# Two-layer decoder trunk, first pass: order of the loads, place of the casts, place of the bias rows

## The chip, the cores and the metric

The kernel runs on one core of one Trainium2 chip. The metric is the device time of one launch in microseconds (us), the median of several runs. The engines of the core are TensorE (PE; its weight loads are PEld), VectorE (DVE), ScalarE (ACT), GpSimd (POOL) and SyncE (SP). SP issues most DMA transfers, GpSimd the others; both kinds run on the core's 16 DMA engines (queue q1 holds SP's, q0 GpSimd's).

## The reference

Two layers, each with a token mixer and a gated convolutional FFN, each sub-layer normed and modulated by vectors that come from a conditioning vector c. The part that matters here is the beginning of layer 0:

```python
mod = jax.nn.silu(c) @ w_ada[0] + b_ada[0]
sh1, sc1, g1, sh2, sc2, g2 = [m[:, None, :] for m in jnp.split(mod, 6, axis=-1)]
h = rmsnorm(x, norm_mix[0]) * (1.0 + sc1) + sh1
qkv = (h @ w_in).reshape(B, S, A_GROUPS, 3, A_HEADS, A_HEAD_DIM)   # 1024 -> 9216
# per group and head: dilated causal attention with a bias that a table
# rel_bias gives by distance; then the mixture of the groups, the output
# projection, the FFN, and layer 1 with gated linear attention
```

There are 256 tokens of width 1024. All is float32.

## The kernel before

Products are made of float32 numbers in three: each operand is split into a high part (a cast to the type that TensorE multiplies fast, on ScalarE) and a low part (the rest, a subtraction on VectorE), and high x high, low x high and high x low are added up in PSUM. A weight chunk is therefore loaded (tile raw), cast (whi), subtracted (wlo), and then multiplied.

The model's width is cut into eight tiles of 128 (kt = 0 to 7). The **first pass** (lines 391 to 478, and the products at 679 to 709) goes over these eight tiles once. For a tile it
- loads the tile's ada chunk (1 MB, two pieces up to kt = 3, else one; L415) and its chunk of w0, the input weights of the first two pairs of heads (0.98 MB, also in two pieces up to kt = 3: 768 and 1152 columns; L418). Chunks of odd tiles go to one fixed room (early_x), all other loads share a ring of four buffers (wraw), so that a load waits on SP until the buffer's last reader is done;
- makes two dot products of the ada chunk with silu(c) on VectorE (L161). On ScalarE the first becomes the scale m1 (L170), the second the shift m0 (L172);
- scales x by m1 and the norm's factor on VectorE (xr, L432), adds m0 on ScalarE, which gives the high part hhi (L436), and takes the low part hlo on VectorE (L440);
- casts w0's two column pieces on ScalarE (L448, the first between m1 and m0, the second behind the high part) and subtracts their low parts on VectorE (L453);
- multiplies on TensorE, 36 products of 256 columns and 6 of 384 (L690, L686), in a written order: high x high first, which needs both casts; the pieces with wlo last.

The order on ScalarE and on VectorE is written out: each step stands behind the one before it (`behind`, with the lists on_act and on_dve; it orders instructions of one engine and adds no wait on another). A tile's steps on VectorE are dot, dot, scale, first low part, hlo, second low part. Where no order is written, a planner sets it before the launch; so it is for SP's queue. What SP and GpSimd issue goes in the order of their queues: an issue that waits for a buffer holds all behind it.

Behind the pass ScalarE and VectorE empty the banks (L597 and L598 the first pair, whose bank TensorE writes next). TensorE goes on with a chunk of query and key weights (wqk, whole products by parts, L654; its casts at L191), then scores, and a chunk of value weights (wv). 

GpSimd builds the table rows of biases (L370); at the end of the pass SP stores it to DRAM (rows_d, L479) and loads the rest of small (L480). From there GpSimd loads each pair of heads' bias, eight copies of 64.5 and 32 KB in turn (L384, L385, in short runs of up to 1 KB); the first two pairs have buffers at once. In its queue behind these stand two room loads (L495) of 1 MB ada chunks for later, to the rooms early_x and x_all, which are free when tile 7's dots and scaling are done. At most eight of GpSimd's transfers are in flight in this stretch.

Of the kernel before, what the change touches and what calls it, by code (L numbers as in the profile page):

```python
# [57 lines left out]
def trunk(ctx: ExitStack, tc: tile.TileContext, I, out):  # L58
    nc = tc.nc
# [12 lines left out]
    def bank(name="ps", tag=None):  # L72
        tag = tag or next(cycle)
        return psum.tile([P, 512], F32, tag=tag, name=name, bufs={"p": 2, "s": 4, "t": 2}[tag])
# [44 lines left out]
    @contextmanager  # L119
    def behind(*those):  # L120

        with ExitStack() as st:
            for i in those:
                st.enter_context(tc.issue_after(i.ins))
            yield
# [29 lines left out]
    def modulation(raw, l, n, order=(0, 1), between=None):  # L155
        first = ()
        for s in order:
            piece, kt = ADA_ORDER[2 * n + s]
            dot = tmp.tile([P, 1], F32, tag="dot", name="dot", bufs=4)
            w = raw[:, D * s : D * s + D]  # L160
            last_dot[0] = nc.vector.tensor_tensor_reduce(  # L161
                w, w, c_bc, op0=ALU.mult, op1=ALU.add, scale=1.0, scalar=0.0, accum_out=dot,
            )
            m = state.tile([P, 1], F32, tag=f"mod{l}{piece}{kt}", name="mod")
            b = col(C_BADA + 48 * l + 8 * piece + kt)
            with behind(*first):
                if piece in (1, 4):
                    g = col((C_NMIX if piece == 1 else C_NFFN) + 8 * l + kt)
                    b1 = (16 if piece == 4 else 0) + 8 * l + kt
                    last = nc.scalar.activation(m, dot, AF.Identity, scale=g, bias=one_b[:, b1 : b1 + 1])  # L170
                else:
                    last = nc.scalar.activation(m, dot, AF.Identity, bias=b)  # L172
            mod[l, piece, kt] = m
            if between and s == order[0]:
                first = between(last)
        return last


    last_load, copied, last_lo = [None], [None], [None]

    def split(src, n, dmas=1, after=((), ()), late=(), low=()):
        raw = wraw.tile([P, 2048], F32, tag="raw", name="raw")
        for i in range(dmas):
            c = slice(n * i // dmas, n * (i + 1) // dmas)
            last_load[0] = nc.sync.dma_start(raw[:, c], src[:, c])
        hi = wspl.tile([P, 2048], F32R, tag="whi", name="whi")
        lo = wspl.tile([P, 2048], F32R, tag="wlo", name="wlo")
        for i in range(0, n, n // 2):
            c = slice(i, i + n // 2)
            with behind(*after[i > 0]):  # L190
                copied[0] = nc.scalar.copy(hi[:, c], raw[:, c])  # L191
        for i in range(0, n, n // 2):
            c = slice(i, i + n // 2)
            with behind(*(late if i else low)):
                last_lo[0] = nc.vector.tensor_tensor(lo[:, c], raw[:, c], hi[:, c].bitcast(F32), op=ALU.subtract)  # L195
        return hi, lo
# [16 lines left out]
    def mm3(ps, a, b, start, stop):  # L213


        mm(ps, a[0], b[0], start=start, stop=False)  # L216
        mm(ps, a[0], b[1], start=False, stop=False)  # L217
        return mm(ps, a[1], b[0], start=False, stop=stop)  # L218
# [137 lines left out]
    def parts(w, at, n=P):  # L356
        return w[0][:, at : at + n], w[1][:, at : at + n]
# [3 lines left out]
    rows_d = dram.tile([16, NROW], F32, name="rows_d")  # L361
# [3 lines left out]
    rows = att.tile([16, NROW], F32, tag="pt", name="rows")  # L365
# [40 lines left out]
    w0, h, xr, raw0 = [], [], [None] * KT, []  # L406
    pieces = (slice(0, 6 * P), slice(6 * P, 15 * P))
    on_act = [norm_ops[1]]

    rooms = [z.rearrange("p k t -> p (k t)")[:, 0:2048] for z in (early_all, x_all)]  # L410

    def load(kt):
        chunk = rooms[0] if kt % 2 else wraw.tile([P, 2048], F32, tag="raw", name="ada_raw")
        for c in (slice(D, 2 * D), slice(0, D)) if kt < 4 else (slice(0, 2 * D),):
            nc.sync.dma_start(chunk[:, c], I["w_ada"][0, kt][:, c])  # L415
        raw = wraw.tile([P, 2048], F32, tag="raw", name="raw")
        for c in pieces if kt < 4 else (slice(0, 15 * P),):
            last_load[0] = nc.sync.dma_start(raw[:, c], I["w0"][kt][:, c])  # L418
        raw0.append(raw)
        w0.append([wspl.tile([P, 2048], F32R, tag=f"w{part}", name=f"w{part}") for part in ("hi", "lo")])  # L420
        return chunk

    def dots(kt, between=None):
        chunk = load(kt)
        with behind(on_dve[0], on_act[0]):
            on_act[0] = modulation(chunk, 0, kt, (1, 0), between)
        on_dve[0] = last_dot[0]

    def scaled(kt):
        xr[kt] = tmp.tile([P, T], F32, tag="xr", name="xr")  # L430
        with behind(on_dve[0]):
            on_dve[0] = nc.vector.scalar_tensor_tensor(xr[kt], x[kt], mod[0, 1, kt][:, 0:1], r, op0=ALU.mult, op1=ALU.mult)  # L432

    def shifted(kt):
        with behind(on_act[0]):
            on_act[0] = nc.scalar.activation(h_hi[kt][:, :], xr[kt], AF.Identity, bias=mod[0, 0, kt][:, 0:1])  # L436
# [8 lines left out]
    def cast(kt, half):  # L445
        c = pieces[half]
        with behind(on_act[0]):
            on_act[0] = nc.scalar.copy(w0[kt][0][:, c], raw0[kt][:, c])  # L448
# [4 lines left out]
            on_dve[0] = nc.vector.tensor_tensor(w0[kt][1][:, c], raw0[kt][:, c], w0[kt][0][:, c].bitcast(F32), op=ALU.subtract)  # L453

    def tile_of(kt):
        def first_cast(last):
            on_act[0] = last
            cast(kt, 0)
            return on_act[:1]

        dots(kt, first_cast)
        scaled(kt)
        shifted(kt)
        cast(kt, 1)

    for kt in range(KT):
        tile_of(kt)
# [8 lines left out]
            low(kt, 1)  # L476
    scale_terms(1)
    with tc.issue_after(last_load[0].ins):
        nc.sync.dma_start(rows_d, rows)  # L479
        nc.sync.dma_start(small[:, C_CW:], I["small"][:, C_CW:])  # L480

    o_hi, o_lo = [], []
# [155 lines left out]
    def queries(u, g, *qk):  # L638
        pq, pk, middle, end = raw_queries(u, g, after=pt_copy[:1] if (u, g) == (3, 0) else ())
        kept[:] = evacuate(*qk, g, pq, pk)  # L640
        with behind(kept[1]):
            room_ada()
        return middle, end

    def raw_queries(u, g, tag="p", low=(), by_parts=False, after=()):
        w = split(I["wqk"][u - 2, g], 2048, low=low, late=low, after=(after, after))
        pqk = bank("pqk", tag)
        pq, pk = pqk[:, :T], pqk[:, T:]
        if by_parts:
            for part in range(3):  # L650
                for kt in range(KT):
                    for i, ps in enumerate((pq, pk)):
                        at = 2 * P * kt + P * i
                        end = mm(ps, w[part == 2][:, at : at + P], h[kt][part == 1], start=(part == kt == i == 0),  # L654
                                 stop=(part == 2 and kt == KT - 1 and i == 1))
            return pq, pk, None, end
        for kt in range(KT):
            s, e = kt == 0, kt == KT - 1
            mm3(pq, parts(w, 2 * P * kt), h[kt], s, False)
            end = mm3(pk, parts(w, 2 * P * kt + P), h[kt], False, e)  # L660
            if kt == 3:
                middle = end
        return pq, pk, middle, end
# [13 lines left out]
    last = [warm]  # L677
# [24 lines left out]
    for kt in range(1, KT):  # L702
# [4 lines left out]
        for part in (1, 2):  # L707
# [3 lines left out]
    qk0, qk1 = new_qk(), new_qk()  # L711
    left = [evacuate(*qk, g, pqk[2 * g], pqk[2 * g + 1])
            for qk, pqk, g in ((qk0, pqk0, 1), (qk0, pqk0, 2), (qk0, pqk0, 0), (qk1, pqk1, 0), (qk1, pqk1, 1), (qk1, pqk1, 2))]
    pq, pk, middle, end = raw_queries(2, 0, tag="t", low=left[2][1:], by_parts=True)
    with behind(left[-1][0], left[-3][0]):
        v0 = by_groups(pv)
    bias = load_bias(0)
# [3 lines left out]
    with behind(end):  # L721
        s, last = scores(*qk0)
# [6 lines left out]
    end = values(1, 1, pv, after=left[-1][:1], low=evacuated[1:])  # L729
# [5 lines left out]
    with behind(end):  # L735
        s, last = scores(*qk1)
    raised = maxima(s, bias1)

    for u in range(2, NPAIR):
# [3 lines left out]
        with behind(last):  # L743
            if u > 2:
                queries(u, 0, *qk)
            middle, end = queries(u, 1, *qk)
# [9 lines left out]
        middle, end = queries(u, 2, *qk)  # L756
# [5 lines left out]
        end = values(u, 0, pv, after=first)  # L762
# [3 lines left out]
        if u < NPAIR - 1:  # L766
            end = values(u, 1, pv)
        with behind(end, turned):
            s, last = scores(*qk)
        with behind(last):  # L770
            last = outputs(u - 1, v, before[1])
# [264 lines left out]
    for n in range(4):  # L1036
# [7 lines left out]
        for i in range(2):  # L1044
            kt = 2 * n + i
            for t in range(2):
                ht = [y[:, P * t : P * t + P] for y in h[kt]]
                for s in range(2):
                    with behind(*last_gate if kt == 5 else ()):
                        last = mm3(pv[t][s], ht, parts(w, D * i + 512 * s, 512), kt == 0, kt == KT - 1)  # L1050
# [18 lines left out]
    def in_turn(products):  # L1069
        with behind(*(run if run[0] else ())):  # L1070
            run[0] = products()
# [288 lines left out]
    with behind(last_pd[0]):  # L1360
        last = mean_square([0])
    with behind(last):
        last = turned(range(2))
    with behind(last):
        last = mean_square([1])
# [7 lines left out]
    for half in range(2):  # L1373
        for t, own in enumerate(halves):
            c = slice(512 * half, 512 * half + 512)
# [118 lines left out]
```

## Time and profile before

| | us |
|---|---|
| median of 3 runs (754.93 to 756.13) | 755.52 |
| the profiled execution | 754.74 |
| its span | 753.0 |
| TensorE busy (share of the span) | 745.0 (99%) |
| weight loads busy | 723.7 (96%) |
| VectorE busy | 630.5 (84%) |
| ScalarE busy | 491.5 (65%) |
| mean DMA rate | 248 GB/s |

The chain that ended last lies 88% on TensorE. The granted clock of TensorE is full throughout (2.4 GHz). A busy TensorE is not a full one: products are pipelined, and a product that waits inside still counts. So the first pass has to be read from the starts of its tiles and from the waits of the weight loads. In the first 50 us the DMA engines are full.

### The profile page before, as it was taken

The page shows a single profiled execution, that of the slowest core. Times are in us where ns is not written, and L with a number is a line of the kernel's source. Part 1 is how long each engine was busy: PE and PEld are TensorE (multiplying, and loading weights), DVE is VectorE, ACT ScalarE, POOL GpSimd, SP SyncE. Part 2 cuts the span into 40 slices and gives each one's busy share as a digit, 9 for nine tenths or more (in the row PEclk, how much of TensorE's full clock was granted, in tenths as well). Part 3 has the DMA queues.
Part 4 walks back from the last instruction along what each step waited for, and adds up shares of the span by engine and source line. Part 5 has one row for each costly group of instructions (what it writes and reads, how often), then busy time and mean ns, then how long its engine had stood idle before and what let it go on. Part 6 is the DMA issues. An engine that isn't in the chain of part 4 may idle for free.

```text
span 753.0 us, 16106 instructions
## 1 busy us (share of the span) xinstructions
PE 745.0 (99%) x6474; PEld 723.7 (96%) x6474; DVE 630.5 (84%) x1124; ACT 491.5 (65%) x954; POOL 78.2 (10%) x148
## 2 busy tenths in 40 slices
PE   9999999999999999999999999999999999999997
PEld 7999999999999999999999998899999999999996
DVE  7988977887978688999988778987897989898672
ACT  6467676576666588676766547845878766666552
POOL 6243320320200010000000002000010000000100
PEclk9999999999999999999999999999999999999999
DMA  8999788888886666866646985873475755556741
GB/s 340 417 353 369 246 297 308 292 280 280 288 282 227 235 224 220 285 225 229 241 147 229 329 315 180 340 277 130 155 279 172 277 188 204 198 181 216 266 149 56
DMA packets 31997, 186.83 MB, mean 248 GB/s; under 512 B 4386, under 2 KB 4770, under 8 KB 16051
## 3 DMA queue, kind: packets, MB, share of 16 engines
q1 hardware_dynamic: 26816, 162.38, 60.0%
q0 software_dynamic: 4784, 23.09, 9.4%
q8 instruction: 50, 0.82, 0.4%
q10 hardware_dynamic: 322, 0.35, 0.1%
q14 instruction: 25, 0.20, 0.1%
HBM read 184.70 MB, written 1.10 MB: 247 GB/s over the span
## 4 chain that ended last, share of the span: by engine, by line
PE 88%; DVE 5%; DMA 3%; ACT 2%; issue 1%; SPq 0%; ACTq 0%; DVEq 0%
PE pab L216 10%; PE pab L217 10%; PE pab L218 10%; PE pd L216 5%; PE pd L217 5%; PE pd L218 5%; PE pqk L216 5%; PE pqk L217 4%; PE pqk L218 4%; PE pv L217 3%; PE pv L218 3%; PE pv L216 3%; DMA early_x<-in_w_ada 2%; PE py L217 2%; PE py L218 2%; PE py L216 2%
## 5 line engine op out<-in xcount | busy, mean ns | idle before, releaser
L195 DVE TENSOR_TENSOR wlo<-raw,whi 128x1024 fp32r<-128x1024 f32 (+3 forms) x254 | 272.4, 1105 | 54.7 <-ACT whi L191 53.6
L191 ACT CAST whi<-raw 128x1024 fp32r<-128x1024 f32 (+3 forms) x254 | 228.6, 949 | 107.4 <-PE pab L217 40.8
L218 PE MATMUL pab<-hhi,wlo 128*128 128x256 f32 x672 | 184.9, 276 | 0.0
L217 PE MATMUL pab<-hlo,whi 128*128 128x256 f32 x672 | 184.8, 277 | 0.0
L216 PE MATMUL pab<-hhi,whi 128*128 128x256 f32 x672 | 183.4, 277 | 0.0
L218 PEld LDWEIGHTS pab<-hhi,wlo 128*128 128x128 f32 x672 | 126.2, 188 | 0.0
L217 PEld LDWEIGHTS pab<-hlo,whi 128*128 128x128 f32 x672 | 126.0, 188 | 0.2
L216 PEld LDWEIGHTS pab<-hhi,whi 128*128 128x128 f32 x672 | 125.2, 188 | 0.1
L217 PE MATMUL pd<-glo,whi 128*128 128x256 f32 x352 | 97.1, 276 | 0.0
L218 PE MATMUL pd<-ghi,wlo 128*128 128x256 f32 x352 | 97.1, 276 | 0.0
L216 PE MATMUL pd<-ghi,whi 128*128 128x256 f32 x352 | 96.8, 276 | 0.0
L216 PE MATMUL pqk<-hhi,whi 128*128 128x256 f32 x314 | 88.2, 281 | 0.0
L217 PE MATMUL pqk<-hlo,whi 128*128 128x256 f32 x314 | 87.0, 277 | 0.0
L218 PE MATMUL pqk<-hhi,wlo 128*128 128x256 f32 x314 | 87.0, 277 | 0.0
L161 DVE CUSTOM_DVE_ANT_0 ada_raw<-ada_raw,c_bc 128x1024 f32<-128x1024 f32 x52 | 61.4, 1222 | 8.2 <-DMA ada_raw<-in_w_ada 8.2
L217 PEld LDWEIGHTS pd<-glo,whi 128*128 128x128 f32 x352 | 66.1, 188 | 0.0
L218 PEld LDWEIGHTS pd<-ghi,wlo 128*128 128x128 f32 x352 | 66.1, 188 | 0.0
L216 PEld LDWEIGHTS pd<-ghi,whi 128*128 128x128 f32 x352 | 65.9, 188 | 0.0
L216 PEld LDWEIGHTS pqk<-hhi,whi 128*128 128x128 f32 x314 | 59.1, 188 | 0.5
L217 PEld LDWEIGHTS pqk<-hlo,whi 128*128 128x128 f32 x314 | 59.0, 188 | 0.0
L218 PEld LDWEIGHTS pqk<-hhi,wlo 128*128 128x128 f32 x314 | 59.0, 188 | 0.0
L897 ACT ACTIVATE r<-pab,small 128x256 f32<-128x256 f32 x86 | 46.8, 561 | 15.7 <-DVE r L900 15.6
(244 smaller groups left out, 1500.8 us busy)
## 6 DMA issues: line engine op xcount, KB each, us to landing
raw<-in_w_up SPq DMA_DIRECT2D x42, 1024.0 KB, 4.8
ada_raw<-in_w_ada SPq DMA_DIRECT2D x24, 1024.0 KB, 5.0
raw<-in_w_down SPq DMA_DIRECT2D x32, 704.0 KB, 5.1
raw<-in_wqk SPq DMA_DIRECT2D x18, 1024.0 KB, 5.8
raw<-in_wv SPq DMA_DIRECT2D x14, 768.0 KB, 6.3
early_x<-in_w_ada POOLq DMA_DIRECT2D x9, 1024.0 KB, 6.6
x_all<-in_w_ada POOLq DMA_DIRECT2D x9, 1024.0 KB, 6.2
raw<-in_w_out_a SPq DMA_DIRECT2D x4, 1024.0 KB, 5.3
```

What stands on the lines that cost most here:

```text
L161: last_dot[0] = nc.vector.tensor_tensor_reduce(w, w, c_bc, op0=ALU.mult, op1=ALU.add, scale=1.0, scalar=0.0, accum_out=dot,)
L191: copied[0] = nc.scalar.copy(hi[:, c], raw[:, c])
L195: last_lo[0] = nc.vector.tensor_tensor(lo[:, c], raw[:, c], hi[:, c].bitcast(F32), op=ALU.subtract)
L216: mm(ps, a[0], b[0], start=start, stop=False)
L217: mm(ps, a[0], b[1], start=False, stop=False)
L218: return mm(ps, a[1], b[0], start=False, stop=stop)
L897: nc.scalar.activation(r, u[:, :T], AF.Identity, scale=cw[2], bias=col(C_CB + 44 * l + f))
```

## The change

Four edits. (1) All loads of the first pass go through in_turn, which puts each behind the one issued before it, so that SP's queue is strictly ada chunk, w0 chunk, tile by tile. (2) The store of rows moves from the end of the pass to behind the loads of tile 5. (3) From kt = 3 on the first cast stands ahead of m1, and the second between m1 and m0; nothing is cast behind the high part. (4) The casts of the first wqk chunk stand behind the last high part on ScalarE.

```diff
+    def in_turn(to, of):
+        with behind(*(last_load if last_load[0] else ())):
+            last_load[0] = nc.sync.dma_start(to, of)
+
     def load(kt):
         chunk = rooms[0] if kt % 2 else wraw.tile([P, 2048], F32, tag="raw", name="ada_raw")
         for c in (slice(D, 2 * D), slice(0, D)) if kt < 4 else (slice(0, 2 * D),):
-            nc.sync.dma_start(chunk[:, c], I["w_ada"][0, kt][:, c])
+            in_turn(chunk[:, c], I["w_ada"][0, kt][:, c])
         raw = wraw.tile([P, 2048], F32, tag="raw", name="raw")
         for c in pieces if kt < 4 else (slice(0, 15 * P),):
-            last_load[0] = nc.sync.dma_start(raw[:, c], I["w0"][kt][:, c])
+            in_turn(raw[:, c], I["w0"][kt][:, c])
+        if kt == 5:
+            in_turn(rows_d, rows)
...
-    def dots(kt, between=None):
-        chunk = load(kt)
+    def dots(kt, chunk, between):
         with behind(on_dve[0], on_act[0]):
             on_act[0] = modulation(chunk, 0, kt, (1, 0), between)
...
     def tile_of(kt):
-        def first_cast(last):
+        def one_cast(last):
             on_act[0] = last
+            cast(kt, int(kt > 2))
+            return on_act[:1]
+
+        chunk = load(kt)
+        if kt > 2:
             cast(kt, 0)
-            return on_act[:1]
-
-        dots(kt, first_cast)
+        dots(kt, chunk, one_cast)
         scaled(kt)
         shifted(kt)
-        cast(kt, 1)
+        if kt < 3:
+            cast(kt, 1)
...
     with tc.issue_after(last_load[0].ins):
-        nc.sync.dma_start(rows_d, rows)
         nc.sync.dma_start(small[:, C_CW:], I["small"][:, C_CW:])
...
-    pq, pk, middle, end = raw_queries(2, 0, tag="t", low=left[2][1:], by_parts=True)
+    pq, pk, middle, end = raw_queries(2, 0, tag="t", low=left[2][1:], by_parts=True, after=on_act)
```

## Rows read from the trace of the kernel before

**Rows 1.** Waits of weight loads, 24.1 to 58.4 us: sum, times, longest

```profile
PEld pqk L690 <- ACT whi L448: 1.4, 5, 0.3
PEld pqk L690 <- ACT hhi L436: 0.7, 1, 0.7
```

**Rows 2.** The same waits from 60 us to the end, longest real one

```profile
PEld pv L217 <- DVE wlo L195: 0.6, 1, 0.6
```

**Rows 3.** Timeline of PE: start, us; tiles 2, 3, 7, next pass

```profile
24.10 1.52 PE L690 MATMUL pqk<-hhi,whi 128*128 128x256 f32 x12
...
29.26 2.02 PE L690 MATMUL pqk<-hhi,whi 128*128 128x256 f32 x12
...
52.76 2.00 PE L690 MATMUL pqk<-hhi,whi 128*128 128x256 f32 x12
...
58.40 1.98 PE L654 MATMUL pqk<-hhi,whi 128*128 128x256 f32 x16
```

**Rows 4.** Timeline of DVE: scaling 3 and 4, second low part 4, evacuation

```profile
28.11 0.48 DVE L432 SCALAR_TENSOR_TENSOR xr<-x_all,mod,rstd 128x256 f32<-128x256 f32 x1
...
33.84 0.48 DVE L432 SCALAR_TENSOR_TENSOR xr<-x_all,mod,rstd 128x256 f32<-128x256 f32 x1
...
36.02 1.36 DVE L453 TENSOR_TENSOR wlo<-raw,whi 128x1152 fp32r<-128x1152 f32 x1 [0.43 <-ACT whi L448]
...
57.44 0.76 DVE L598 COPY k<-pqk 128x256 f32<-128x256 f32 x2 [2.30 <-ACT q L597]
```

**Rows 5.** Timeline of ACT: tile 4, next pass' casts, evacuation

```profile
32.82 0.39 ACT L170 ACTIVATE mod<-dot,one_b,small 128x1 f32<-128x1 f32 x1 [2.57 <-DVE dot L161]
33.11 0.83 ACT L448 CAST whi<-raw 128x768 fp32r<-128x768 f32 x1
...
34.42 0.51 ACT L436 ACTIVATE hhi<-xr,mod 128x256 fp32r<-128x256 f32 x1 [0.16 <-DVE xr L432]
...
53.66 3.47 ACT L191 CAST whi<-raw 128x1024 fp32r<-128x1024 f32 x4
57.02 0.65 ACT L597 ACTIVATE q<-pqk 128x256 f32<-128x256 f32 x2
```

**Rows 6.** Timeline of SP: issues of loads (two merged: first to last)

```profile
17.69 0.80 SPq L418 DMA_DIRECT2D raw<-in_w  x2
...
22.48 3.78 SPq L418 DMA_DIRECT2D raw<-in_w  x2
28.22 0.33 SPq L415 DMA_DIRECT2D early_x<-in_w_ada  x1
...
40.26 0.33 SPq L415 DMA_DIRECT2D early_x<-in_w_ada  x1
43.70 0.33 SPq L185 DMA_DIRECT2D raw<-in_wqk  x1
```

**Rows 7.** DMA issues at 18.1, 22.4, 40.2, 43.6: KB, us to landing

```profile
raw<-in_w SPq DMA_DIRECT2D x1, 576.0 KB, 10.1
...
raw<-in_w SPq DMA_DIRECT2D x1, 960.0 KB, 10.5
...
early_x<-in_w_ada SPq DMA_DIRECT2D x1, 1024.0 KB, 8.2
...
raw<-in_wqk SPq DMA_DIRECT2D x1, 1024.0 KB, 8.1
```

**Rows 8.** Timeline of POOL: first bias copy, first room load

```profile
45.78 0.69 POOL L384 DMA_DIRECT2D bias<-rows_d  x1 [21.62 <-DMA rows_d<-rows]
...
58.44 0.57 POOL L495 DMA_DIRECT2D early_x<-in_w_ada  x1 [0.50 <-DVE k L598]
```

**Rows 9.** Busy time of engines, 30 to 40 us; last: DMA share, GB/s

```profile
30.00:40.00 10.00, 9.85 (x75) 9.33 (x75) 8.81 (x12) 4.10 (x8) 0.00 (x0) 1.00 1.02 418
```

**Rows 10.** DMA queues, 49 to 59 us: packets, MB, share of 16 engines

```profile
q1 hardware_dynamic: 350, 2.14, 68.7%
q0 software_dynamic: 388, 0.61, 26.4%
```

## The prediction

> **What bounds the kernel now.** I read the waits first, then each engine's timeline of the first pass (8.7 to 58.4 us), then the DMA issues and their landings. TensorE's weight loads wait for almost nothing after 60 us [rows 2], so a gain or loss of the first pass reaches the end one to one, unless the loads behind it fall late. Inside the pass they wait for the casts (1.4 us over five tiles) and for one late high part (0.7) [rows 1]. A tile that never waits takes TensorE 24.10 to 29.26 = 5.16 us; the last one takes 52.76 to 58.40 = 5.64 [rows 3]. Five tiles without waits after 29.26 would end at 55.06: 3.34 us is all there is to win.
>
> What paces the tiles is VectorE: from scaling to scaling 28.11 to 33.84 = 5.73 us, and 0.43 of it is the wait of the second low part for the second cast [rows 4]. Behind it stands the DMA: it moves 418 GB/s without a gap [rows 9], so a 1.05 MB ada chunk costs 2.5 us and 0.98 MB of w0 2.35, 4.85 for a tile. All three, TensorE at 5.16, VectorE and DMA, are within 0.6 us of one another.
>
> **Casts ahead, tiles 3 to 7.** No instruction is added; ScalarE's order becomes first cast, m1 (the scale term), second cast, m0 (the shift term), high part. With the loads there, m1 still follows the first dot (32.82 in tile 4), the second cast takes the slot that the first has now (33.11), 1.05 us to the next issue, then m0 0.30, so the high part starts at 34.46 against 34.42 [rows 5]: 0.04 later. VectorE's 0.43 us at the second low part is gone, TensorE's 0.3 at the second cast too. VectorE's period becomes about 5.3, and TensorE at 5.16 becomes the limit.
>
> But ScalarE now holds m1 behind a cast that needs w0's load. In tile 3 the second piece, issued at 18.2 [rows 6], lands 10.1 us later [rows 7], at 28.3: second cast 28.3, high part 29.65 to 30.15, TensorE 30.2 instead of 29.26. VectorE waits for that high part and comes to tile 4 some 0.3 us late. In tile 4 w0 lands at 22.48 + 10.5 = 33.0 [rows 6, 7]: first cast 33.0, m1 33.75, second cast 34.05, high part 35.4 instead of 34.42, TensorE 35.96. These two tiles are about 1 us late, but run through in 5.16. Tile 5 follows at TensorE's pace at 41.15, tile 6 at 46.35, tile 7 at 51.55 against 52.76, if its loads are there.
>
> The Trainium skill speaks against this part (DMA: Bandwidth & Descriptors, Rules for kernel authors): issue a transfer early, do other work, and wait for it late; here the wait moves ahead. The rows of tiles 3 and 4 agree with it. By the rule alone, with tile 4's 0.98 us never won back, the sum would be +1.0.
>
> **Loads strictly by tile.** Up to w0 of tile 4 the queue is by tile already; then w0 5 (the second of the two at 22.48) goes ahead of ada 5 (28.22), and w0 7, rows and small go ahead of ada 7 (40.26) [rows 6]. In the new order w0 5 stands behind ada 5, whose buffer is free only after tile 3's dots (28.11 [rows 4]): issued 28.2 and 28.55 instead of 25.9. The DMA doesn't run dry, since w0 4 lands at 33.0. From there by bytes: ada 5 35.5, where it was 37.8 (so TensorE's 0.7 us of rows 1 is gone), w0 5 37.85, rows 38.0, ada 6 40.5, w0 6 42.85, ada 7 45.35, w0 7 47.7. Ada 7 may go at 40.0, when tile 5's dots end, and w0 7 behind it. Tile 7's dots start at 48.1, and its first cast must start by 48.4 if m1 isn't to slip. So w0 7 has 0.7 us to spare, and without any other traffic the pass ends at 51.55 + 5.2 = 56.75, 1.65 us early.
>
> **Rows behind tile 5's load.** This moves more than one store. GpSimd has waited 21.62 us for rows; its bias copies go the moment it lands, at 45.78 [rows 8], just before the pass's last load (ada 7: 40.26 + 8.2 = 48.5 [rows 6, 7]), and GpSimd's queue moves its first packets from 49 on (the window of rows 10), some 4 us after that issue. With rows landed at 38.0 the first copy goes at 38.3 and the packets of both units flow from 42 to about 51.5: beside w0 6, ada 7 and w0 7. Their price is in the row of 49 to 59 us: 26.4% of ten us on all DMA engines, 2.64 us [rows 10]. One landing shows it: wqk came 43.70 + 8.1 = 51.8 [rows 6, 7], 3.3 us after ada 7, where its bytes take 2.5: 0.8 late, some 2.5 us into the flow. W0 7 ends some 8 us into the flow, so it is between 1.9 us late (the 0.79 MB of sixteen copies, 64.5 and 32 KB in turn, at 418 GB/s) and 3.1 (the share, with the 4.9% in which neither queue moved). I take 2.6, the row of the share: w0 7 lands at 50.3. Then the last first cast starts at 50.3, m1 0.75 on, second cast 0.29 on, m0 1.05 on, high part 0.30 on, done after 0.55: TensorE at 53.25, end 58.45. The whole gain is eaten: +0.05 us, with -0.65 and +0.55 as ends.
>
> **Next pass' casts behind the last high part, and who else comes early.** The wqk casts already run after the last cast, four casts in a row from 53.66 with those of the first wv, and the evacuation of the banks follows at 57.02 [rows 5]; TensorE goes on at 58.40 [rows 3]. The chain as such costs nothing: the high part is late anyway. But both loads stand behind w0 7 on SP's queue: 50.3, small 0.4, wqk 2.5, wv 1.9: wqk 53.2, wv 55.1. And the two 1 MB room loads of GpSimd, which wait behind sixteen bias copies and go at 58.44 now [rows 8], wait in the new kernel only for tile 7's dots and scaling: 51.0 and 52.4. If the first flows from 52 on (an estimate: 1 us behind its issue; the small copies took 4), SP then has 0.18 + 1.05 + 0.79 less the 0.7 since 50.3 = 1.3 MB to move (the rest of wqk, and wv): alone 3.1 us (wv 55.1), at half the rate 6.2 (58.2). Not shown by any row of before is how the two queues share there; I take the middle, 56.7. The second wv cast is then done 56.7 + 1.65 = 58.35, and the first evacuated pair, which frees the bank that TensorE writes next, 0.85 later: 59.2. (ScalarE's half begins at 57.02 [rows 5], VectorE's at 57.44 and takes about 0.4 of its 0.76 for two [rows 4]: 57.87 in the kernel before, in time for TensorE at 58.40.)
>
> **The sum.** 59.2 against 58.40 is +0.8 us. The profiled execution took 754.74 us (span 753.0) and the median of the three runs is 755.52, 0.78 above; the difference is added to the median: 756.3. Ends of the unknown prices: w0 7 0.7 earlier and no sharing, -0.65; w0 7 0.5 later and half the rate, +2.8.
>
> **Rivals.**
> *The design works.* Bias copies spread thin enough beside queued loads that w0 7 lands by 48.4. For it: the DMA didn't slow before the copies' packets came, 4 us after the issue, and if those waited longer behind a full SP queue the last load would be through. Against it: the 0.8 us of wqk. It gives -1.65, at most -2.2: 753.9.
> *The room loads take half of the DMA* (the other side). Place: wv's landing ahead of the evacuation on ScalarE. Price: 58.2 + 1.65 + 0.85 = 60.7, +2.3, and with w0 7 at 50.8 +2.8: 757.8 and 758.3. It decides from wv landing later than 55.9 on (58.40 - 0.85 - 1.65). By a page of the Trainium skill this would be the case (DMA: Bandwidth & Descriptors, Queues, rings and completion order): each DMA engine serves its queues in turn, packet by packet. No row of before has both queues full with large packets throughout, so the trace neither bears it out nor refutes it.
> *Evacuation unhindered.* The scheduler sets wv's casts behind the evacuation, or wv is there in time: +0.05, 755.6.
> *The edit does nothing to loads or copies*, because SP or GpSimd keeps another order: then only the casts count, -0.5 to +1.0.
>
> **How the numbers follow.** Forecast (+0.8, own range -0.2 to +1.7) 0.33; design works 0.26; half rate 0.22; evacuation unhindered 0.14; nothing moved 0.05. Predicted 756.3. The range reaches over the design's centre and the half rate's, 753.7 to 758.3. A measurement of this kernel tells about 0.2% (1.5 us) from no change. Faster takes three fifths of the design's case and some of the tails, 0.20; slower takes most of the half rate's and a part of the forecast's, 0.31; the same 0.49.
>
> **What would show it.** After: no wait of L453 for L448 in tiles 3 to 7; TensorE's tile 3 and 4 start near 30.2 and 36.0; rows issued near 29, first bias copy near 38.3; w0 7 landing near 50.3; high part 7 near 53.2; room loads near 51 and 52.4; ScalarE idle ahead of L191 or L597 for a DMA. I'm wrong if the bias copies don't start before 42, if w0 7 lands before 48.5, or if TensorE waits in the next stages.

## The result and the profile after

| | us |
|---|---|
| kernel before, median (754.93 to 756.44) | 755.83 |
| changed kernel, median (760.43 to 762.46) | 760.62 |
| ratio | 1.0078 [1.0062, 1.0094] |
| the profiled execution of the changed kernel | 762.46 (span 760.6) |

The changed kernel is 0.78% slower: 5.9 us by the ratio, 4.8 by the two medians. In a second comparison, of other runs, the ratio was 1.0081 [1.0067, 1.0095], 6.1 us. The forecast was 756.3 with 753.7 to 758.3, so the time lies outside the range, on its slow side. The lines of the changed kernel are shifted: the high part is L441, w0's casts L453, its low parts L458, the products L698 and L694, the next pass L662, the evacuation L605 and L606, the copies out of the values bank (the PSUM bank that the products with wv fill) L620 to L623, the exponentials of the attention (Exps) L559, the room loads L503.

TensorE's waits between 24 and 90 us in the changed kernel (sum, times, longest):

```profile
PE pqk L698 <- ACT hhi L441: 2.7, 2, 2.4
PE pqk L216 <- ACT v L623: 2.1, 1, 2.1
```

The waits for casts of [rows 1] are gone, as meant. In their place stand one long wait for a high part, and one that the prediction has no line for, behind the pass. Busy time by slices of 10 us in the changed kernel (PE, PEld, DVE, ACT, POOL, then PEclk, DMA share, GB/s):

```profile
40.00:50.00 10.00, 10.00 (x83) 9.94 (x83) 10.00 (x15) 3.66 (x8) 6.44 (x12) 1.00 1.04 309
50.00:60.00 10.00, 7.65 (x49) 7.45 (x48) 3.69 (x7) 5.64 (x9) 1.70 (x3) 0.83 1.01 356
60.00:70.00 10.00, 10.00 (x110) 9.66 (x110) 7.61 (x16) 9.10 (x23) 0.20 (x2) 1.00 0.96 361
70.00:80.00 10.00, 8.58 (x84) 7.73 (x82) 9.62 (x19) 4.47 (x12) 5.19 (x11) 1.00 0.74 230
```

Three things are to be seen: the DMA engines are full at 40 to 50 us, yet move 309 GB/s (it was 418 in [rows 9], and 411 at 40 to 50 us in the kernel before); TensorE's granted clock is 0.83 at 50 to 60; and TensorE is busy for only 7.65 and 8.58 us in two of the slices. The timeline of PE shows where (start, duration; tiles 3, 4, 5 and 6, then tile 7 to the next pass):

```profile
29.83 1.68 PE L698 MATMUL pqk<-hhi,whi 128*128 128x256 f32 x12
...
35.73 1.65 PE L698 MATMUL pqk<-hhi,whi 128*128 128x256 f32 x12 [0.34 <-ACT hhi L441]
...
41.01 1.52 PE L698 MATMUL pqk<-hhi,whi 128*128 128x256 f32 x12
...
46.20 1.64 PE L698 MATMUL pqk<-hhi,whi 128*128 128x256 f32 x12
...
53.98 1.86 PE L698 MATMUL pqk<-hhi,whi 128*128 128x256 f32 x12 [2.35 <-ACT hhi L441]
55.64 2.76 PE L698 MATMUL pqk<-hlo,whi 128*128 128x256 f32 x12
58.20 0.74 PE L694 MATMUL pqk<-whi,hhi 128*128 128x384 f32 x2
...
60.88 2.05 PE L662 MATMUL pqk<-hhi,whi 128*128 128x256 f32 x16
```

TensorE stood idle for 2.35 us ahead of tile 7, and then ran twelve products in 2.76 us that take 1.52 at the full clock. A narrower window shows the granted clock there, 0.50, the lower of its two levels (1.2 of 2.4 GHz); 0.83 over ten us is that level for about a third of them:

```profile
56.00:58.00 2.00, 2.00 (x12) 2.00 (x11) 0.00 (x0) 1.67 (x2) 0.00 (x0) 0.50 1.04 422
```

Tile 7 takes 53.98 to 60.88 = 6.9 us instead of 5.2. ScalarE shows what it waited for, and what holds the second wait:

```profile
51.03 0.83 ACT L453 CAST whi<-raw 128x768 fp32r<-128x768 f32 x1 [4.88 <-DMA raw<-in_w]
...
53.42 0.51 ACT L441 ACTIVATE hhi<-xr,mod 128x256 fp32r<-128x256 f32 x1
55.68 1.99 ACT L191 CAST whi<-raw 128x1024 fp32r<-128x1024 f32 x2 [1.75 <-DMA raw<-in_wqk]
59.22 0.39 ACT L605 ACTIVATE q<-pqk 128x256 f32<-128x256 f32 x1 [1.55 <-PE pqk L698]
59.50 1.56 ACT L191 CAST whi<-raw 128x768 fp32r<-128x768 f32 x2
...
75.01 0.29 ACT L172 ACTIVATE mod<-dot,small 128x1 f32<-128x1 f32 x1 [4.66 <-DVE dot L161]
...
76.36 1.03 ACT L191 CAST whi<-raw 128x1024 fp32r<-128x1024 f32 x1
77.30 0.61 ACT L559 ACTIVATE prob<-prob,m 128x384 f32<-128x384 f32 x1
...
78.51 1.03 ACT L191 CAST whi<-raw 128x1024 fp32r<-128x1024 f32 x1
79.44 0.36 ACT L620 COPY v<-pv 64x256 f32<-64x256 f32 x1
```

w0 7 lands at 51.0. Later the copies that empty the second values bank stand behind two shift terms, two casts and two Exps, and start at 79.44. In the kernel before they start at 73.58:

```profile
72.14 0.62 ACT L551 ACTIVATE prob<-prob,m 128x384 f32<-128x384 f32 x1
...
73.36 0.28 ACT L172 ACTIVATE mod<-dot,small 128x1 f32<-128x1 f32 x1
73.58 0.37 ACT L612 COPY v<-pv 64x256 f32<-64x256 f32 x1
```

There, too, two Exps and a shift term stand ahead of them, but these wait for nothing. In the changed kernel ScalarE stands idle for 4.66 and 0.85 us ahead of the two shift terms, for dots that VectorE makes only at 73.75 to 76.04, and the copies stand behind. TensorE needs that bank for the next queries and waits 2.1 us (first the kernel before, then the changed one):

```profile
75.52 0.38 PE L216 MATMUL pqk<-hhi,whi 128*128 128x256 f32 x1
```

```profile
80.78 0.38 PE L216 MATMUL pqk<-hhi,whi 128*128 128x256 f32 x1 [2.14 <-ACT v L623]
```

Set against the kernel before, TensorE is 2.48 us late at the next pass (60.88 against 58.40 of [rows 3]), 3.05 at the second unit's scores, and 5.45 behind the second wait. That stays, within half a us, until 704 us. This execution lost 2.1 us more behind that; a second profile of the same kernel ended at +6.2.

### The profile page after: what moved, and what is told of

Same layout as the page of the kernel before. It is cut to its first block, busy times and chain, and to the rows that moved or that the text cites. A ratio compares the mean times of both kernels' runs of the same rounds, so it can differ in the third digit from the quotient of the medians.

```text
span 760.6 us, 16105 instructions
## 1 busy us (share of the span) xinstructions
PE 748.1 (98%) x6474; PEld 727.5 (96%) x6474; DVE 630.4 (83%) x1124; ACT 489.9 (64%) x954; POOL 77.9 (10%) x148
## 4 chain that ended last, share of the span: by engine, by line
PE 86%; DVE 6%; DMA 4%; ACT 3%; issue 1%; ACTq 0%; DVEq 0%
PE pab L216 10%; PE pab L217 10%; PE pab L218 10%; PE pd L218 5%; PE pd L217 5%; PE pd L216 5%; PE pqk L216 5%; PE pqk L217 4%; PE pqk L218 4%; DMA raw<-in_w 3%; PE pv L217 3%; PE pv L218 3%; PE pv L216 2%; PE py L217 2%; PE py L218 2%; PE py L216 2%
```

## The experiments

Ratios are to the kernel before in the same rounds; 0.001 is 0.75 us.

### One part at a time

**Casts ahead alone** (edits 3 and 4 on the kernel before).

```diff
         chunk = load(kt)
+        if kt > 2:
+            cast(kt, 0)
...
-        cast(kt, 1)
+        if kt < 3:
+            cast(kt, 1)
```

> The kernel before with one edit alone: casts ahead of scale and shift from tile 3 on (and the next casts behind the last high part). Theory: VectorE's wait at the second low part goes; ada 7 lands at 48.5 as before and now bounds tile 7's dots, which started at 49.33: TensorE starts tile 7 about 0.9 us earlier and runs it in 5.2; 754.5 to 755. Rival A: 758 or more.

0.9996 [0.9987, 1.0005]. Tiles 3 to 7 start at 30.65, 36.55, 41.88, 47.16 and 52.36, the next pass at 57.78: 0.62 us earlier than in [rows 3]. Tiles 3 and 4 are late, and the period of 5.2 to 5.3 us afterwards wins it back. Tile 7 starts 0.40 us earlier, where 0.9 was expected. So this part does what it says, and it is worth less than the measurement can tell.

**Loads in turn alone** (edit 1 on the kernel before, rows at the end).

> The kernel before with one edit alone: the loads of the first pass strictly by tile, rows at the end. Theory: the 0.5 us wait for ada 5 goes, the rest keeps VectorE's pace of 5.73 us a tile; 755.3. Rival B: 757.5 or more, with ScalarE or VectorE waiting for w0 5 or w0 7.

1.0053 [1.0035, 1.0071]: the time that Rival B gave, but not by its waits, since neither ScalarE nor VectorE waits for a load in the pass. The pass itself ends 0.33 us earlier. The loss is behind it: TensorE waits for the copies of the second values bank, which the planner had put behind four Exps, and the granted clock falls (a line of PE's timeline, and the slice):

```profile
77.00 0.58 PE L216 MATMUL pqk<-hhi,whi 128*128 128x256 f32 x1 [1.73 <-ACT v L619]
```

```profile
70.00:80.00 10.00, 8.28 (x80) 7.75 (x79) 10.00 (x24) 7.19 (x20) 3.33 (x8) 0.85 0.96 330
```

**Rows early alone** (edit 2 on the kernel before).

```diff
+        if kt == 5:
+            with behind(ada, last_load[0]):
+                nc.sync.dma_start(rows_d, rows)
```

> The kernel before with one edit alone: the store of rows stands behind the loads of tile 5. Theory: the bias copies start near 38, their packets run beside ada 7, which lands 2 to 3 us later than 48.5; tile 7 starts 2 us later, the room loads start near 52 and the next loads of the ring come late; 758 to 760 us. Rivals A and B: no change, 755.8.

1.0048 [1.0036, 1.006]. The first product of tile 7, and its slice:

```profile
55.41 2.01 PE L692 MATMUL pqk<-hhi,whi 128*128 128x256 f32 x12 [2.34 <-ACT hhi L439]
```

```profile
50.00:60.00 10.00, 7.57 (x58) 7.18 (x57) 5.40 (x8) 6.44 (x10) 2.20 (x4) 1.00 1.03 346
```

The next pass begins at 61.05, 2.65 us late, with no second wait. Here ada 7 is the last load; it lands 11.5 us after its issue, 8.2 in [rows 7]. So this edit alone makes the first loss. The clock kept its upper level here after an idle time as long as that of the changed kernel.

**All but the rows** (the changed kernel with the store back at the end).

```diff
-        if kt == 5:
-            in_turn(rows_d, rows)
...
     with tc.issue_after(last_load[0].ins):
+        nc.sync.dma_start(rows_d, rows)
```

> The changed kernel with one edit undone: the store of rows stands at the end of the pass again. Theory (the early bias copies and, behind them, the early room loads take the DMA from the last loads): the first bias copy goes near 48, w0 of tile 7 lands near 47.7, tile 7 starts near 51.5 on TensorE, the next pass near 56.8, 1.6 us ahead of the kernel before; about 754.1 us. Rival A (the casts ahead make ScalarE wait for w0's load and that is the loss): no better than 759. Rival B (the strict order of the loads delays w0 5 and 7): no better than 758.

0.9994 [0.9983, 1.0004]. Two lines of PE's timeline, the next pass and the values bank:

```profile
56.34 1.98 PE L661 MATMUL pqk<-hhi,whi 128*128 128x256 f32 x16
```

```profile
74.12 0.38 PE L216 MATMUL pqk<-hhi,whi 128*128 128x256 f32 x1 [0.59 <-ACT v L622]
```

The pass ends 2.06 us earlier than before: this is the forecast's "design works", and more. But a third of it goes at the values bank.

### The second wait

**Values first**: the changed kernel, with the copies of the second values bank ahead of the mods (the shift terms), the Exps and the last wqk casts on ScalarE.

```diff
+        v_copy[0] = copy(v[top, 2 * P : 3 * P], pv[low, P : 2 * P])
...
+    with behind(last_max[0], v_copy[0]):
+        room_ada()
+    with behind(v_copy[0]):
+        before = probabilities(*raised)
```

> The changed kernel, with one more order: on ScalarE the copies of the second values bank out of PSUM come ahead of room ada's products, the Exps and the casts of the last wqk tile (as they stood ahead of most of these in the kernel before). Theory A (three separate losses: 2.35 us idle at tile 7, a lower granted clock for some microseconds behind it, and a second stall of 2.1 us near 78 us that the planner's new order on ScalarE makes): the first pass stays as in the changed kernel (TensorE starts tile 7 at 54, reaches the next pass at 60.9), the wait of the queries' products for the values bank goes, and the kernel is 2 to 2.4 us faster than the changed one, about 2.6 us (ratio 1.0035) slower than the kernel before. Theory B (the second stall comes from wqk and wv tiles that land late because the room loads run beside them): TensorE waits as long, for another tile; ratio 1.006 or more.

1.0053 [1.004, 1.0066] against 1.0078 and 1.0081. TensorE has no wait at the values bank any more, and the 1.9 to 2.1 us that the kernel won are what the wait had been. The expected 1.0035 was not reached. The first pass is unchanged:

```profile
54.16 2.93 PE L700 MATMUL pqk<-hhi,whi 128*128 128x256 f32 x12 [2.60 <-ACT hhi L441]
56.88 1.79 PE L700 MATMUL pqk<-hlo,whi 128*128 128x256 f32 x12
...
60.94 1.98 PE L664 MATMUL pqk<-hhi,whi 128*128 128x256 f32 x16
```

The same order was put into two other kernels.

> The kernel before with its loads in strict order alone (rows at the end, casts in their old places), and the copies of the second values bank first on ScalarE. Loads in order alone had been 1.0053 [1.0035, 1.0071], with a stall of 1.9 us behind those copies and a clock of 0.85 behind it. Theory A (that loss was the planner's new order on ScalarE, and not the loads' order): no stall and no fall of the clock near 75 us, and the 0.33 us that the first pass gave back remains: ratio 0.999 to 1.0. Theory B (the order of the loads makes the weights behind the pass late): 1.003 or more.

0.9997 [0.9988, 1.0005], where loads in turn alone had been 1.0053: no wait, no lower clock, the pass's small gain kept. So that loss was the planner's order on ScalarE and not the loads.

> The changed kernel with the rows stored at the end of the first pass's loads as in the kernel before, and the copies of the second values bank ahead of the other work on ScalarE. Theory A: the first pass ends 2.06 us earlier than before, as it did with the rows at the end alone, and the 0.7 us that TensorE then waited for the values bank goes too: 1.9 to 2.1 us faster than the kernel before, ratio 0.9974. Theory B: the time that the first pass gives back is lost again at the next tiles of weights, whatever ScalarE's order: ratio 0.9994 as with the rows at the end alone.

0.9982 [0.9972, 0.9992]: faster than the kernel before and than the changed kernel, by 1.4 and about 7 us. In its profiled execution the next pass begins at 57.10, 1.30 us early (2.06 with the rows at the end alone), and this comes through to the end (span 751.7 us, 753.0 before).

The changed kernel itself was run again beside some of these:

> The changed kernel as it is, once more, on the chip and in the rounds of the three runs below, so that each can be set against it. The same ratio as before, 1.0062 to 1.0094, and the same two stalls: over 2 us at tile 7 behind hhi, and some 2 us near 78 us behind the copies of the second values bank.

1.0081, with waits of 2.81 and 2.03 us at the two places.

### The first wait: the store, the copies, or the room loads

**Copies behind w0 7**: values first and rows early, but GpSimd reads one column of w0 7 ahead of the bias copies.

```diff
+    seen = const.tile([P, 1], F32, name="seen")
+    with behind(nc.gpsimd.tensor_copy(seen[:, :], raw0[7][:, 0:1])):
+        bias = load_bias(0)
```

> The kernel with the values copies first and the rows stored early as in the changed kernel, but GpSimd reads one column of w0 7's raw tile ahead of the bias copies, so that they are issued when it has landed. It tells the early store of the rows from the copies that it lets loose. Theory A (only the copies' packets make w0 7 late): w0 7 lands some 7.5 us after its issue and not 11, near 47.7; TensorE waits under 0.5 us at tile 7, and the first pass ends 2.5 us or more earlier than with the values copies first alone, as with the rows at the end: ratio 0.997 to 0.9995, if the copies' new place starts no other wait. Theory B (the 48 KB of the rows in the weights' own queue cost the time): it lands at 50 or later, ratio 1.004.

0.9984 [0.9976, 0.9993]; the next pass begins at 56.24. The DMA queues at 40 to 51 us (packets and mean rate, then queue: packets, MB, share of 16 engines; last the load of w0 7, KB, us to landing), first in the changed kernel, then here:

```profile
DMA packets 877, 3.38 MB, mean 308 GB/s; under 512 B 240, under 2 KB 368, under 8 KB 709
q1 hardware_dynamic: 525, 2.82, 82.1%
q0 software_dynamic: 352, 0.56, 20.5%
...
raw<-in_w SPq DMA_DIRECT2D x1, 960.0 KB, 10.7
```

```profile
DMA packets 749, 4.22 MB, mean 384 GB/s; under 512 B 84, under 2 KB 212, under 8 KB 492
q1 hardware_dynamic: 748, 4.22, 96.4%
...
raw<-in_w SPq DMA_DIRECT2D x1, 960.0 KB, 7.2
```

The rows are stored early in both. The store costs nothing; the copies that it lets loose make w0 7 3.5 us late. They hold the engines for 20.5% of 11 us = 2.3 us, and SP's packets are slower beside them: 2.82 MB in 82.1% of 11 us is 0.31 MB per us, without the copies 4.22 MB in 96.4% is 0.40. The two room loads stand behind the copies and move with them (58.52 instead of 51.05), but they don't make w0 7 late: in the changed kernel they are issued when it has landed.

**Half the copies**: values first, with the second unit's eight copies held back.

> The kernel with the values copies first, in which only the first unit's bias copies are issued beside the first pass's last loads; the second unit's stand behind a memset that GpSimd does later. It tells whether the bias copies' number sets w0 7's lateness. Theory A (each copy's packets take turns of the DMA engines from w0 7): w0 7 lands near 49.4 and not at 51.0, TensorE waits some 0.8 us at tile 7 and not 2.35, its granted clock stays at the upper level, and the kernel is 2.5 to 3.5 us faster than the one with the values copies first, within 0.7 us of the kernel before. Theory B (w0 7 is late for its place in its own queue, or for the rows' store): it lands at 51 as with all copies, and the time is the same as with the values copies first.

1.0025 [1.0013, 1.0037], 2.1 us faster than with all copies. The size missed: w0 7 still lands at 51.1 (9.9 us after its issue, which came 0.9 later in this execution), and TensorE waits 1.56 us at tile 7, at the full clock. Against the 7.2 us without copies, the first eight cost w0 7 some 2.7 us, and the second eight, issued from 43.6 on, 0.5 to 1.4 more (10.7 us in the changed kernel, 11.3 with the values first, 10.5 and 10.4 in the two kernels with fillers below). What counts is what flies while w0 7 is under way.

**Room loads held** (56 memsets ahead of them on GpSimd; they were issued at 61.2 and 61.8 instead of 51.3 and 53.1).

> The kernel with the values copies first, and GpSimd kept busy between its bias copies and the two room loads by 56 memsets of a pad (about 6 us), so that the room loads are issued near 57 us and not at 51. It tells what the room loads' place beside the last weights costs. Theory A (they cost nothing on the path once ScalarE's order is mended): the same time as the kernel with the values copies first, within 0.5 us. Theory B (they make the late wqk and wv tiles late, and these set TensorE's next waits): 1 to 2 us faster than it.

1.0047 [1.0029, 1.0064], the same as values first; a cost of 1 us could hide in the two intervals. The traces say more: the second wv tile lands 12.5 us after its issue instead of 16.2, so the room loads do make it late, but TensorE reaches the scores 5.53 us behind the start of the next pass in both (61.72 to 67.25, 60.94 to 66.47). There the room loads' early place costs nothing.

### The clock

**Fillers**: values first, with 18 products of zeros between tile 6 and tile 7, which add zero.

```diff
+        if kt == 7:
+            with behind(*last):
+                for _ in range(18):
+                    last[0] = mm(pqk1[5], zero[:, :], h[6][0][:, :], start=False, stop=False)
```

> The kernel with the values copies first, and 18 products of a block of zeros (they add zero to a bank that accumulates) on TensorE between tile 6 and tile 7, in the 2.6 us in which it waits there. At 0.12 us each they fill about 2.1 us of the wait and put nothing off. It measures the clock's part of the loss. Theory A (the granted clock falls because TensorE stands idle): no slice under 1.00 at 50 to 60 us, tile 7 takes 5.3 us and not 6.8, and the next pass begins 1.4 to 1.7 us earlier than with the values copies first alone (59.4 against 60.9): ratio about 1.003. Theory B (the clock falls for something else that happens there, such as ScalarE's casts and the loads): 0.83 again in that stretch, and the time of the values copies first, 1.005.

1.0062 [1.0047, 1.0078]. The clock did stay at 1.00, and tile 7 ran from 54.45 to about 59.85, 5.4 us instead of 6.8. But the planner had put the evacuation behind the first wv casts, and the wait and the lower clock (0.83 again, at 60 to 70) came there (ScalarE's line, then PE's):

```profile
60.28 1.56 ACT L191 CAST whi<-raw 128x768 fp32r<-128x768 f32 x2 [1.80 <-DMA raw<-in_wv]
```

```profile
62.64 3.43 PE L664 MATMUL pqk<-hhi,whi 128*128 128x256 f32 x16 [2.64 <-DVE k L606]
```

**Fillers, evacuation first**: the same, with the first evacuated bank ahead of those casts.

```diff
-        values(1, 0, pv, low=left[-1][1:])
+        values(1, 0, pv, after=left[0][:1], low=left[-1][1:])
```

> The kernel with the values copies first and the 18 products of zeros between tile 6 and tile 7, in which ScalarE evacuates the first queries bank ahead of the casts of the first wv tile, as it does without the fillers. In the run with the fillers alone the planner had put that evacuation behind those casts, and TensorE waited 2.64 us for it at the next pass, at a clock of 0.83 in the slice behind. Theory A (a wait of 2 us and more on TensorE costs its length and then 1.4 us of lower clock): no wait for the evacuation, no slice under 1.00 from 50 to 80 us, next pass at 59.3 to 59.9, and 1.2 to 1.7 us faster than the values copies first without fillers (1.0053): ratio 1.003 to 1.004. Theory B (the clock's fall only moves to a later place): a slice under 1.00 further on and 1.005 again.

1.0056 [1.0043, 1.007], not 1.003 to 1.004. The clock is 1.00 from 50 to 100 us, and the next pass begins 1.39 us earlier than with the values first (59.55 against 60.94). It is lost at once: ScalarE waits for wv until 59.95, the second evacuation stands behind those casts, VectorE's low parts of wqk behind the evacuation, and TensorE behind these:

```profile
64.31 2.33 PE L664 MATMUL pqk<-hhi,wlo 128*128 128x256 f32 x16 [0.97 <-DVE wlo L195]
```

The lower clock is a cost of 1.4 us at its place, but here it lay beside a wv tile that was late anyway. Taking it away moved the end by nothing that can be measured.

## Why the prediction was wrong

The sum let the copies eat the gain of the pass, and put the loss at one place: +0.8 us at the next pass, where TensorE would wait for the evacuation. That wait didn't come. In its place stand a higher price of the copies for w0 7, a lower clock for tile 7 and a wait at the values bank; the sum had the first too small and the other two at nothing.

**Right.** The casts: no waits of low parts for casts, tile 3 late at 29.83 (forecast 30.2), tile 4 at 35.73 (35.96), made good at 41.01 (41.15) and 46.20 (46.35). The Trainium skill (DMA: Bandwidth & Descriptors, Rules for kernel authors) advises to issue a transfer early and to wait for it late. The trace shows the lateness that waiting early brings (tile 4 at 35.73), and also that it was won back, which the forecast's +1.0 "by the rule alone" didn't allow. Casts and loads in order together were worth what the sum said: without the copies in their way the pass ends at 56.34, 56.24 and 57.10 in three kernels, forecast 56.75. GpSimd went when the sum said it would (timelines of SP and POOL: rows, w0 7, first bias copy, room loads):

```profile
29.51 0.38 SPq L414 DMA_DIRECT2D rows_d<-rows  x1
...
40.20 0.55 SPq L414 DMA_DIRECT2D raw<-in_w  x1
```

```profile
38.03 0.69 POOL L384 DMA_DIRECT2D bias<-rows_d  x1 [13.88 <-DMA rows_d<-rows]
...
51.05 0.57 POOL L503 DMA_DIRECT2D early_x<-in_w_ada  x1 [0.24 <-DMA bias<-rows_d]
52.96 0.54 POOL L503 DMA_DIRECT2D x_all<-in_w_ada  x1 [1.35 <-DVE xr L437]
```

The forecast had 29, 38.3, 51.0 and 52.4 for rows, copies and room loads. That the copies eat the gain of the pass was the right mechanism too. One reading was off without consequence: the paces of TensorE, VectorE and DMA (5.16, 5.73 and 4.85 us) lie within 0.9 us, not 0.6.

**Mis-sized: the price of the copies for w0 7.** The step took 2.6 us (1.9 to 3.1); it was 3.5. It came from the share of the copies' queue [rows 10], their own time on the engines. Two things were missing. The packets began about 2 us after the issue and not 4: at 40 to 42 us GpSimd's queue has 37.9% of the engines, so all of w0 7's 10.7 us lay in their flow. And SP's packets beside them were slower by more than the turns taken (0.31 MB per us of their share against 0.40). [rows 10] had this already: 2.14 MB in 68.7% of ten us is 0.31 MB per us as well, and the forecast put it at nothing. The Trainium skill (DMA: Bandwidth & Descriptors, Queues, rings and completion order) says that each DMA engine serves its queues in turn, packet by packet. The trace agrees in so far as both queues move packets side by side; why SP's packets take longer beside the small ones isn't shown. This term moved tile 7 from 53.25 to 53.98.

**Missing: the lower clock behind the idle time.** The sum let tile 7 run in 5.2 us behind a wait of 1.7 us (51.55 to 53.25). It waited 2.35 us and then ran, in part at the lower granted clock, in 6.9: the pass ended at 60.88 instead of 58.45, 0.7 of it from w0 7 and 1.7 from tile 7, of which the clock is 1.4 to 1.6 (tile 7 at the full clock took 5.3 us with half the copies and 5.4 with fillers).

**Not there: the wait for the evacuation.** The forecast's +0.8 at the next pass, and the rival of the room loads with +2.3 to +2.8, rested on wv's casts standing ahead of the evacuation. The planner put the first evacuation ahead (59.22 and 59.50 in the lines above), and TensorE went on without a wait: on this point the rival "evacuation unhindered" was right. The place is real, though: where the planner did set the casts ahead, in the first run with fillers, it cost 2.64 us, with wv landing at 60.3, later than the half rate's 58.2. Room loads do make the second wv tile late (16.2 us from issue to landing, 12.5 with them held), but holding them changed nothing in the time.

**Missing: the planner.** The prediction read each queue past which a load was moved, but took ScalarE's order behind the pass as given. The edits name no instruction there; still the copies of the values bank, at 73.58 in the kernel before, came to 79.44, behind casts, Exps and two shift terms that wait for VectorE. That is 1.9 to 2.1 us of the 5.9, and with the loads in turn alone it is all of the loss. The forecast's first paragraph let a loss of the first pass reach the end "one to one, unless the loads behind it fall late"; here the order of another engine changed instead. Its last sentence (wrong "if TensorE waits in the next stages") named the sign, but it had no price and no chance in the sum.

**The account.** From the changed kernel's 1.0078 and 1.0081, the values bank's order takes it to 1.0053, and the copies' place from there to 0.9984 (5.2 us, of which 4.7 show at the next pass, 60.94 against 56.24: the wait at tile 7 and the lower clock behind it). What remains is the gain of the other edits, 1.2 us. **Open**: the whole time of some kernels is further from before than their traces are (values first +2.1 us in its profile, +4.0 by the ratio; its profiled execution was the fastest of six). Two traces show a place where executions differ. In the changed kernel, behind a wait of 0.31 us at 711.56, TensorE does 87 products in ten us to the end, where it did 91 in the kernel before, both at the full granted clock (the kernel before, then the changed one):

```profile
720.00:730.00 10.00, 10.00 (x91) 10.00 (x90) 6.12 (x9) 4.84 (x9) 0.00 (x0) 1.00 0.56 192
```

```profile
720.00:730.00 10.00, 10.00 (x87) 10.00 (x86) 5.10 (x9) 4.35 (x9) 0.65 (x1) 1.00 0.64 236
```

That is 1.5 of the 2.1 us that this execution lost there. The profile of the copies behind w0 7, the slowest execution of its eleven, has the same from 705 us on. Why, and whether the executions without a trace lost theirs so, isn't shown. Open too is why the copies' packets came 2 us after their issue here and about 3 us or more in the kernels with the rows at the end.

## What to carry to other kernels

Moving a small transfer earlier moves everything that waits for it: list what its landing sets free, and price many short packets beside a queue of large ones by what the large ones lose, not by the short ones' bytes or time alone. Where a planner sets the order, any edit can move work in stages that it doesn't touch; compare the order behind the edit, and write down an order for instructions that free a bank the critical engine writes next. Waits lie in layers: take one away and see the next before adding up prices (here the last weight, the clock and the next weight).

## What the runs showed of the hardware

- The granted clock of TensorE fell to 0.83 in the slice with, or just behind, idle times of 2.35, 2.60, 2.64, 2.81 and 2.98 us, and to 0.85 behind one of 1.73; it stayed at 1.00 with idle times of 2.34 (rows early alone), 2.14 and 2.03 (the second wait of the changed kernel, in its two profiles) and 1.56 (half the copies). So the length of one wait doesn't decide alone, and what does isn't shown. At tile 7, 1.4 to 1.6 us of TensorE's time hung on it.
- DMA engines that are full by their share can move much less: 308 GB/s at 40 to 51 us with the bias copies among the weights, 384 without them (at a share of 96%), 418 in [rows 9].
- 18 products of zeros (2.2 us) in the idle gap at tile 7 kept the clock at 1.00 there, in two kernels.
- At the full granted clock TensorE did 91 products at 720 to 730 us in the kernel before's execution and 87 in the changed kernel's, in the latter behind a wait of 0.31 us.
